# In the first stage of layer 0, the second parts of 31 weight blocks by accumulating DMA in place of subtractions on the vector engine and Pool

## The chip, the cores and the metric

One core of one Trainium2 chip runs the whole kernel in one launch. The metric is the device time of a launch in microseconds; smaller is better. The engines are named as in the profile: PE (matmuls), PEld (its weight loads), DVE (vector engine), ACT (scalar engine), POOL (GpSimd) and SP, which here only issues DMAs.

## The reference

A two-layer decoder step in float32 for a prompt group (512 tokens) and a sample group (8 x 4 tokens) with shared weights, width 1024. What matters here is the first part of layer 0 and the memory keys and values:

```python
def _conformer_conv(u, buf, w_in, b_in, dw, dw_b, ln_g, ln_b, w_out):
    h = jnp.einsum('bld,de->ble', u, w_in) + b_in               # 1024 -> 2048
    g = h[..., :D_MODEL] * jax.nn.sigmoid(h[..., D_MODEL:])
    padded = jnp.concatenate([buf.astype(g.dtype), g], axis=1)
    c = lax.conv_general_dilated(padded, dw[:, None, :], ...) + dw_b   # causal, depthwise, 31 taps
    ...                                                          # LayerNorm of c -> n
    s = jax.nn.silu(n).astype(u.dtype)
    return jnp.einsum('bld,de->ble', s, w_out), padded[:, -CONV_BUF:]

def _mem_kv(mem, w_k, w_v):                                      # 256 memory rows, per layer
    k = jnp.einsum('bmd,de->bme', mem, w_k)
    v = jnp.einsum('bmd,de->bme', mem, w_v)
```

After it come cross-attention and an MLP, then layer 1 (a state-space mixer, attention, MLP) and a final norm. None of that is touched.

## The kernel before

**Precision.** Products are made in fp32r. Each operand is split in two parts: `h`, its fp32r rounding, and `l`, what the rounding left over. A product is three passes over PE: h·h, l·h and h·l (weights named first). So a weight block that arrives by DMA as 128x1024 float32 (512 KB) needs two tiles of the same size before PE can finish with it.

**Blocks and buffers.** All weights are cut in such blocks. SP loads them in the order of use into six staging tiles `wst` (`load_upto`, line 162). `prep_block` makes both parts into one of only three tiles `whl` (128 x 2 x 1024): ACT copies `wst` into the first half (line 168 through the helper on line 136; the first part), then DVE, or Pool for the blocks in the set `lpool`, subtracts: second half = `wst` minus first half (line 172; the second part). A tile `whl` is free again when PE has finished the block that used it. So while PE works on block n, block n+1 is ready or nearly so, and block n+2 is prepared into the tile that block n-1 left.

**The first stage.** It runs from the start to about 240 us and consumes in this order: `in` 0 and 8 (first projections); `k` 0 to 2 (memory keys); then for i = 1 to 7 the pair `a`i, `b`i (blocks `in` i and `in` 8+i, 48 matmuls of 272 columns each); then `k` 3 to 7 (24 matmuls of 256 columns) and eight `v` blocks (12 matmuls of 512 columns), named here v00 to v03 and v10 to v13; then the output projection `cout`. The order is written out by hand in the string `PLAN`. Between those blocks stand:

- `g`i: DVE reads the two PSUM results (lines 520, 522), ACT takes the sigmoid, DVE multiplies, SP stores.
- The depthwise convolution. Channel tiles 0, 3 and 6 are done on DVE (31 operations of 0.77 us each, line 697), handed out in small portions between the other steps. Tiles 1, 2, 4, 5 and 7 are done on PE as banded matrix products: four steps a tile (`10`, `11`, ... `73`, 18 short matmuls each, line 677). Pool builds the band matrix of the step after next (line 650), ACT moves each step's result out of PSUM (line 136). All four results of a tile lie in one PSUM bank, `aux[1]`. Pool adds the finished tiles up (line 619); those of PE first go through DRAM (`ud`, `yd`).
- `L1` to `L3`: a LayerNorm over channels. PE sums (709), DVE subtracts the mean (718), ACT squares, DVE and Pool add the squares (730, 724), PE sums again with a few columns (282), woven between the matmuls of v blocks, DVE takes the reciprocal root (311 to 320), PE spreads it (328).

Each engine runs its own instructions in the order in which the program issues them. An engine that waits holds up all that stands behind it. Of SP, ACT and Pool, the three that issue DMAs, this holds for their DMAs too.

Of the kernel before, what the change touches and what calls it, by code (L numbers as in the profile page):

```python
# [7 lines left out]
F32R = mybir.dt.float32r  # L8
I32 = mybir.dt.int32
AF = mybir.ActivationFunctionType  # L10
ALU = mybir.AluOpType
# [37 lines left out]
BLOCK = {b: i for i, b in enumerate(block_order())}  # L49
# [8 lines left out]
class Trunk:  # L58
# [13 lines left out]
    def __init__(self, nc, tc, pool, psum, I, O):  # L72
        self.nc, self.tc, self.I, self.O = nc, tc, I, O
        self.pool, self.psum = pool, psum
        t = lambda name, *shape: pool.tile([P, *shape], F32, name=name)
# [27 lines left out]
        self.late = []  # L103
        self.lpool = {("k", 0, o) for o in range(1, 3)} | {("v", 0, 0, 3)} | {("v", 0, 1, k) for k in range(4)} | {("cout", o) for o in range(2)}
        self.lpool |= {b for b in self.KV1[1] + self.KV1[2][:2]}


    def ring(self, d):
# [56 lines left out]
    def prep_block(self, b, i, eng=None):  # L165
        t = self.whl.popleft()
        src = self.wst[i % self.NST]
        self.act(t[:, 0].bitcast(F32R), src, AF.Copy)
        if eng is None:
            eng = self.nc.gpsimd if b in self.lpool else self.nc.vector  # L170
        self.hl[b] = t
        eng.tensor_sub(t[:, 1].bitcast(F32R), src, t[:, 0])  # L172

    def pop_all(self):
# [2055 lines left out]
```

## Time and profile before

| | |
|---|---|
| time, median of 3 runs (lowest, highest) | 1548.17 us (1548.09, 1550.21) |
| time of the profiled execution | 1549.96 us |
| its span | 1548.2 us |
| busy: PE, PEld | 1498.7 us, 1452.3 us |
| busy: DVE, ACT, POOL | 1031.3 us, 672.1 us, 193.3 us |
| second parts by DVE, whole span | 149 of 128x1024, 1262 ns mean |
| second parts by Pool, whole span | 19, 2385 ns mean |
| weight loads from SP | 231 of 512 KB, median 4.3 us from issue to landing |

The span is the profiled execution as the trace sees it; 1.8 us of its time lie around it. Busy PE is pipelined time: matmuls overlap, so a busy PE can still be slower than its peak. Idle time in brackets in a timeline row is the idle time of that engine just before the row, with what released it.

### The profile page before, as it was taken

How to read it: one execution, taken by the hardware profiler on the slowest of the kernel's cores; microseconds unless marked ns; L12 is line 12 of the kernel's file. 1: busy time of each engine (PE TensorE's matmuls, PEld its weight loads, DVE VectorE, ACT ScalarE, POOL GpSimd, SP SyncE). 2: the span in 40 equal slices, each digit the busy share in tenths (PEclk: the TensorE clock that was granted, in tenths of full speed). 3: DMA queues.
4: the chain of work that ended last, by engine and by line, in shares of the span. 5: the costliest groups of instructions: out<-in, count | busy, mean ns of one | idle time of the engine just before them, and what ended most of it. 6: DMA issues, size and time to landing. Idle time of an engine off the chain costs nothing.

```text
span 1548.2 us, 29378 instructions
## 1 busy us (share of the span) xinstructions
PE 1498.7 (97%) x11949; PEld 1452.3 (94%) x11949; DVE 1031.3 (67%) x2106; ACT 672.1 (43%) x1262; POOL 193.3 (12%) x155
## 2 busy tenths in 40 slices
PE   8999979999999999999999999999999999999996
PEld 8999969988999999999998889998899999999996
DVE  6997877544577666666756974553479677585855
ACT  6122354333345433565434443343357445272542
POOL 2545451000000000000102760000000000000001
PEclk9999989999999999999999999999999999999998
DMA  7333425363323434333577975336322414141211
GB/s 277 123 90 106 141 112 203 141 256 123 107 73 102 148 134 133 134 133 107 178 259 230 323 241 199 110 137 252 143 69 82 137 55 150 43 140 52 90 47 59
DMA packets 90809, 218.21 MB, mean 141 GB/s; under 512 B 12305, under 2 KB 42785, under 8 KB 86577
## 3 DMA queue, kind: packets, MB, share of 16 engines
q1 hardware_dynamic: 87440, 211.06, 40.1%
q10 hardware_dynamic: 3168, 5.18, 0.9%
q8 instruction: 94, 1.54, 0.4%
q14 instruction: 43, 0.34, 0.1%
q0 software_dynamic: 64, 0.08, 0.0%
HBM read 186.48 MB, written 29.80 MB: 140 GB/s over the span
## 4 chain that ended last, share of the span: by engine, by line
PE 81%; DVE 12%; DMA 2%; issue 2%; ACT 2%; POOL 2%; SPq 0%; DVEq 0%; POOLq 0%; ACTq 0%
PE banks L210 45%; PE banks L1398 12%; PE banks L1290 10%; DVE banks L697 2%; PE banks L462 2%; PE banks L951 2%; PE banks L887 2%; DMA wst<-in_w 1%; PE banks L677 1%; PE banks L445 1%; DVE whl L172 1%; PE banks L968 1%; PE banks L871 1%; PE banks L222 1%; PE banks L1377 1%
## 5 line engine op out<-in xcount | busy, mean ns | idle before, releaser
L210 PE MATMUL banks<-slot,whl 128*128 128x272 f32 x6264 | 803.6, 289 | 5.5 <-ACT slot L136 2.3
L210 PEld LDWEIGHTS banks<-slot,whl 128*128 128x128 f32 x6264 | 792.6, 188 | 10.6 <-issue 4.1
L136 ACT ACTIVATE whl<-wst 128x1024 fp32r<-128x1024 f32 (+1 forms) x236 | 218.7, 931 | 133.4 <-PE banks L1398 47.8
L172 DVE TENSOR_TENSOR whl<-wst,whl 128x1024 fp32r<-128x1024 f32 x149 | 187.5, 1262 | 96.7 <-ACT whl L136 94.0
L1398 PE MATMUL banks<-slot,whl 128*128 128x272 f32 x912 | 120.2, 288 | 0.5 <-DVE rt L1311 0.5
L136 ACT ACTIVATE slot<-banks 128x512 fp32r<-128x512 f32 (+7 forms) x132 | 60.3, 480 | 137.8 <-PE banks L210 42.2
L1398 PEld LDWEIGHTS banks<-slot,whl 128*128 128x128 f32 x912 | 116.7, 188 | 0.7 <-DVE rt L1311 0.7
L1290 PE MATMUL banks<-slot,whl 128*128 128x272 f32 x756 | 97.2, 288 | 0.9 <-DVE tmp L1408 0.9
L1290 PEld LDWEIGHTS banks<-slot,whl 128*128 128x128 f32 x756 | 95.6, 188 | 1.1 <-ACT whl L136 1.1
L136 ACT ACTIVATE slot<-x,vec 128x544 fp32r<-128x544 f32 (+2 forms) x50 | 35.2, 728 | 109.0 <-DVE x L2022 44.2
L1408 DVE TENSOR_TENSOR tmp<-banks,rb 128x544 f32<-128x544 f32 x30 | 21.7, 724 | 83.0 <-PE banks L1398 83.0
L1398 PE MATMUL banks<-slot,arena_mlp 128*128 128x272 f32 x528 | 71.5, 288 | 0.4 <-DVE rt L1311 0.4
L697 DVE SCALAR_TENSOR_TENSOR banks<-slot,vec,banks 128x512 f32<-128x512 f32 x90 | 67.9, 754 | 2.6
L1398 PEld LDWEIGHTS banks<-slot,arena_mlp 128*128 128x128 f32 x528 | 68.2, 188 | 0.6 <-DVE rt L1311 0.6
L1480 POOL MEMSET slot<- 128x128 f32 x1 | 0.2, 205 | 546.9 <-PE banks L1290 546.9
L1290 PE MATMUL banks<-slot,arena_mlp 128*128 128x272 f32 x504 | 65.3, 288 | 0.4 <-DVE acc L1325 0.4
L1290 PEld LDWEIGHTS banks<-slot,arena_mlp 128*128 128x128 f32 x504 | 63.9, 188 | 0.7 <-DVE acc L1325 0.6
L136 ACT ACTIVATE tmp<-x 128x544 f32<-128x544 f32 x40 | 25.9, 648 | 65.0 <-DVE x L1094 39.7
L136 ACT ACTIVATE tmp<-banks 128x544 f32<-128x544 f32 x32 | 19.9, 623 | 76.5 <-PE banks L210 76.5
L420 POOL TENSOR_TENSOR slot<-slot,slot 128x512 fp32r<-128x512 f32 x4 | 6.1, 1559 | 371.4 <-ACT slot L136 371.4
L677 PE MATMUL banks<-slot,arena_mem 128*128 128x128 f32 (+2 forms) x360 | 46.1, 285 | 6.4 <-POOL arena_mem L650 3.3
L172 POOL TENSOR_TENSOR whl<-wst,whl 128x1024 fp32r<-128x1024 f32 x19 | 45.2, 2385 | 55.9 <-ACT whl L136 55.9
(281 smaller groups left out, 2030.4 us busy)
## 6 DMA issues: line engine op xcount, KB each, us to landing
wst<-in_w SPq DMA_DIRECT2D x231, 512.0 KB, 4.3
arena_att<-in_kc SPq DMA_DIRECT2D x16, 1024.0 KB, 4.8
arena_att<-in_vc SPq DMA_DIRECT2D x16, 1024.0 KB, 5.3
tab<-arena_prep SPq DMA_DIRECT2D x24, 512.0 KB, 3.9
arena_s<-tab SPq DMA_DIRECT2D x8, 768.0 KB, 5.5
arena_s<-tab SPq DMA_DIRECT2D x8, 512.0 KB, 6.3
arena_s<-tab SPq DMA_DIRECT2D x12, 256.0 KB, 5.5
x<-in_x SPq DMA_DIRECT2D x8, 272.0 KB, 6.0
```

The source lines that it names most:

```text
L136: self.nc.scalar.activation(out, in_, func, **kw)
L172: eng.tensor_sub(t[:, 1].bitcast(F32R), src, t[:, 0])
L210: self.nc.tensor.matmul(ps[:, c, :HALF], w, x[:, c * HALF : c * HALF + HALF], start=first and n == 0, stop=last and n == len(seq) - 1)
L222: self.nc.tensor.matmul(ps[:, c, :HALF], self.w8(b, kt)[wi], rhs[kt][xi].bitcast(F32R)[:, c * HALF : c * HALF + HALF], start=first and kt ...
L462: nc.tensor.matmul(ps[m], self.memt(2 * kp + k2, xi)[:, m * 128 : m * 128 + 128], t[:, wi, k2 * 512 : k2 * 512 + 512], start=kp == 0 and k ...
L677: nc.tensor.matmul(o[:, s:], mat(n)[:, s * 128 : s * 128 + 128], x[:, : 128 - s], start=s == 0, stop=s == 8)
L697: nc.vector.scalar_tensor_tensor(A, win(k), w(k), A, op0=ALU.mult, op1=ALU.add)
L887: nc.tensor.matmul(o, qs[qi], ks[ki], start=e == 0 and i == 0, stop=e == 1 and i == 2)
L951: nc.tensor.matmul(ps[e], vs[vi], xs[xi], start=m == 0 and i == 0, stop=m == 1 and i == 2)
L1290: nc.tensor.matmul(bank, u[:, wi, k * 128 : k * 128 + 128], x[k][xi].bitcast(F32R), start=n == k == 0, stop=n == 2 and k == 3)
L1398: nc.tensor.matmul(ps[:, c, :HALF], us[kt // 4][:, wi, kt % 4 * 128 : kt % 4 * 128 + 128], M["h"][kt][xi].bitcast(F32R)[:, c * HALF : c * ...
L1408: job("V", 0.7, lambda: V.tensor_mul(self.c2(t), self.psv(ps), self.c2(self.rb)), [*bk, "rb"], [("t", o % 2)])
```

## The change

For 31 blocks (the 14 `in` blocks of the pairs, `k` 1 to 7, all eight `v` blocks of layer 0 and `cout` 0 and 1) the subtraction is gone. In its place ACT writes the negated first part into the second half of the tile, and a DMA that Pool issues reads the block from DRAM a second time and adds it there: second half = -h + w. Of the 31, 22 were subtracted by DVE and 9 by Pool. `in` 0, `in` 8 and `k` 0 stay with DVE, and so does every block after `cout` 1.

```diff
@@ __init__
+        self.ldma = {("in", i + 8 * g) for i in range(1, 8) for g in range(2)} | {("k", 0, o) for o in range(1, 8)}
+        self.ldma |= {("v", 0, n, k) for n in range(2) for k in range(4)} | {("cout", o) for o in range(2)}
@@ prep_block
         self.hl[b] = t
+        if b in self.ldma:
+            self.act(t[:, 1].bitcast(F32R), t[:, 0], AF.Copy, scale=-1.0)
+            self.nc.gpsimd.dma_start(t[:, 1].bitcast(F32R), self.I["w"][BLOCK[b]], accum_op=ALU.add)
+            return
         eng.tensor_sub(t[:, 1].bitcast(F32R), src, t[:, 0])
```

Six lines are added above `tensor_sub` and two of them in `__init__`, so line numbers of the new kernel are larger by 2 up to there and by 6 behind it: 172 becomes 178, 650 becomes 656, and the new DMA is line 176.

How this moves instructions is shown at three places. The first is DVE between `g`2 and `g`3, about 68 to 84 us in the trace. Line 697 is the convolution of tile 0, 633 and 636 sum its sample columns, 520 and 522 open `g`3. Before:

```order
L633 TENSOR_REDUCE slot_798<-slot_632 128x16
L633 TENSOR_REDUCE slot_798<-slot_633 128x16
L636 TENSOR_SCALAR slot_631<-slot_798,vec 128x4x8
L697 SCALAR_TENSOR_TENSOR banks<-slot_496,vec,banks 128x512 x3
L172 TENSOR_TENSOR whl_83<-wst_80,whl_83 128x1024
L697 SCALAR_TENSOR_TENSOR banks<-slot_496,vec,banks 128x512 x7
L633 TENSOR_REDUCE slot_874<-tmp_86 128x16
L633 TENSOR_REDUCE slot_874<-tmp_87 128x16
L636 TENSOR_SCALAR slot_554<-slot_874,vec 128x4x8
L172 TENSOR_TENSOR whl_81<-wst_75,whl_81 128x1024
L520 TENSOR_TENSOR slot_932<-banks,rb 128x544
L522 TENSOR_TENSOR slot_931<-banks,rb 128x544
```

DVE at the same place in the changed kernel:

```order
L639 TENSOR_REDUCE slot_806<-slot_638 128x16
L639 TENSOR_REDUCE slot_806<-slot_639 128x16
L642 TENSOR_SCALAR slot_637<-slot_806,vec 128x4x8
L703 SCALAR_TENSOR_TENSOR banks<-slot_500,vec,banks 128x512 x10
L639 TENSOR_REDUCE slot_883<-tmp_86 128x16
L639 TENSOR_REDUCE slot_883<-tmp_87 128x16
L642 TENSOR_SCALAR slot_559<-slot_883,vec 128x4x8
L526 TENSOR_TENSOR slot_942<-banks,rb 128x544
L528 TENSOR_TENSOR slot_941<-banks,rb 128x544
```

Both subtractions have left DVE's queue; nothing else moved.

The second place is Pool from the last but one addition of a convolution tile (`acc`) on, about 174 to 204 us; line 650 builds a band matrix. Before:

```order
L619 TENSOR_TENSOR acc_84<-acc_84,slot88_1303 128x544
L650 TENSOR_TENSOR arena3072_mem_208<-istk_64,slot31_233 128x1152
L619 TENSOR_TENSOR acc_84<-acc_84,slot95_1452 128x544
L650 TENSOR_TENSOR arena3072_mem_208<-istk_64,slot31_233 128x1152
L172 TENSOR_TENSOR whl0_81<-wst3_78,whl0_81 128x1024
L172 TENSOR_TENSOR whl1_82<-wst4_79,whl1_82 128x1024
L172 TENSOR_TENSOR whl2_83<-wst5_80,whl2_83 128x1024
L714 MEMSET slot119_1956 128x256
```

Pool at the same place in the changed kernel; the DMAs are, from the top, those of `k` 6, `k` 7, v00, v01, v02, v03, v10 and v11:

```order
L176 DMA whl1_82<-in_w 128x1024
L625 TENSOR_TENSOR acc_84<-acc_84,slot88_1317 128x544
L656 TENSOR_TENSOR arena3072_mem_208<-istk_64,slot31_233 128x1152
L625 TENSOR_TENSOR acc_84<-acc_84,slot95_1468 128x544
L176 DMA whl2_83<-in_w 128x1024
L656 TENSOR_TENSOR arena3072_mem_208<-istk_64,slot31_233 128x1152
L176 DMA whl0_81<-in_w 128x1024
L176 DMA whl1_82<-in_w 128x1024
L176 DMA whl2_83<-in_w 128x1024
L176 DMA whl0_81<-in_w 128x1024
L176 DMA whl1_82<-in_w 128x1024
L176 DMA whl2_83<-in_w 128x1024
```

The DMA of `k` 7 stands behind two additions and a build, and that of v00 behind another build; `k` 6, `k` 7 and v00 to v02 were subtracted by DVE before, so Pool had no part in them.

The third place is ACT in the LayerNorm, about 195 to 204 us, where the copy of block v12 stands between the two halves of the squares (`acc` and `slot`). Before:

```order
L136 ACTIVATE whl2_83<-wst5_80 128x1024
L136 ACTIVATE acc_84<-slot50_554 128x544
L136 ACTIVATE slot112_1949<-slot56_631 128x544
L136 ACTIVATE slot113_1950<-slot64_778 128x544
L136 ACTIVATE slot114_1951<-slot72_955 128x544
L136 ACTIVATE whl0_81<-wst0_75 128x1024
L136 ACTIVATE slot115_1952<-slot79_1135 128x544
L136 ACTIVATE slot116_1953<-slot88_1303 128x544
```

ACT at the same place in the changed kernel:

```order
L138 ACTIVATE whl2_83<-wst5_80 128x1024
L138 ACTIVATE whl2_83<-whl2_83 128x1024
L138 ACTIVATE acc_84<-slot50_559 128x544
L138 ACTIVATE slot112_1976<-slot56_637 128x544
L138 ACTIVATE slot113_1977<-slot64_786 128x544
L138 ACTIVATE slot114_1978<-slot72_965 128x544
L138 ACTIVATE whl0_81<-wst0_75 128x1024
L138 ACTIVATE whl0_81<-whl0_81 128x1024
L138 ACTIVATE slot115_1979<-slot79_1147 128x544
L138 ACTIVATE slot116_1980<-slot88_1317 128x544
```

Each copy of a weight block is now followed by a negation, ahead of the squares.

## Rows read from the trace of the kernel before

**Rows 1.** Busy time of each engine in the stretch from the start of `a`1 to `k` 3: stretch, length, busy us and instruction counts, then the granted PE clock (1.00 is 2.4 GHz), the DMA share and GB/s.

```profile
36.80:161.90 125.10, 118.64 (x943) 118.03 (x944) 112.27 (x145) 26.59 (x39) 62.53 (x38) 0.98 0.34 103
```

**Rows 2.** Timeline of PE alone: start, length, instruction, and in brackets the idle time ahead of it. L677 is a step of the convolution on PE, L445 a `k` block.

```profile
63.86 2.24 PE L677 MATMUL banks<-slot,arena_mem 128*128 128x128 f32 x18 [0.55 <-ACT slot L136]
...
80.08 2.16 PE L677 MATMUL banks<-slot,arena_mem 128*128 128x128 f32 x18
84.81 3.67 PE L677 MATMUL banks<-slot,arena_mem 128*128 128x128 f32 x18 [2.56 <-issue]
...
137.85 2.27 PE L677 MATMUL banks<-slot,arena_mem 128*128 128x128 f32 x18 [0.97 <-POOL arena_mem L650]
...
158.58 3.34 PE L677 MATMUL banks<-slot,arena_mem 128*128 128x128 f32 x18 [2.32 <-POOL arena_mem L650]
161.59 3.69 PE L445 MATMUL banks<-arena_mem,whl 128*128 128x256 f32 x24
...
167.04 3.06 PE L445 MATMUL banks<-arena_mem,whl 128*128 128x256 f32 x24
```

**Rows 3.** Timeline of all engines ahead of the two longest of these idle times: a subtraction and the opening of `g`3 on DVE, its sigmoid on ACT, and the moving of step `13` out of PSUM; then the opening of `g`7 and the moving of step `51`.

```profile
81.44 1.54 DVE L172 TENSOR_TENSOR whl<-wst,whl 128x1024 fp32r<-128x1024 f32 x1 [0.33 <-ACT whl L136]
...
82.91 0.71 DVE L520 TENSOR_TENSOR slot<-banks,rb 128x544 f32<-128x544 f32 x1
...
83.70 0.75 ACT L136 ACTIVATE slot<-slot,vec 128x544 f32<-128x544 f32 x1 [2.29 <-issue]
...
84.36 0.35 ACT L136 ACTIVATE slot<-banks,slot 128x128 f32<-128x128 f32 x1
...
156.68 0.72 DVE L520 TENSOR_TENSOR slot<-banks,rb 128x544 f32<-128x544 f32 x1
...
158.09 0.35 ACT L136 ACTIVATE slot<-banks,slot 128x128 f32<-128x128 f32 x1
```

**Rows 4.** Groups of instructions by line in the first 240 us: busy us, mean ns of one, idle time before them. The first two are the copies and DVE's subtractions of weight blocks, the third Pool's subtractions, the last one of the two DMAs that Pool issues in this kernel (64 KB, 128 rows), as long as it held Pool.

```profile
L136 ACT ACTIVATE whl<-wst 128x1024 fp32r<-128x1024 f32 x35 | 36.9, 1054 | 20.7 <-DMA wst<-in_w 7.1 <-issue 6.6 <-PE banks L462 4.4
L172 DVE TENSOR_TENSOR whl<-wst,whl 128x1024 fp32r<-128x1024 f32 x26 | 36.1, 1387 | 14.2 <-ACT whl L136 14.2
...
L172 POOL TENSOR_TENSOR whl<-wst,whl 128x1024 fp32r<-128x1024 f32 x9 | 21.4, 2380 | 35.4 <-ACT whl L136 35.4
...
L372 POOL DMA_DIRECT2D ident<-in_ident x1 | 0.7, 707 | 0.8 <-POOLq L2207 0.8
```

**Rows 5.** The loads of weight blocks (512 KB) in the first 240 us: time from issue to landing.

```profile
DMA to landing us min/median/max: 3.3/4.5/7.0
```

**Rows 6.** DMA issues over the whole span: loads of cached keys, 1024 KB each, median us from issue to landing.

```profile
arena_att<-in_kc SPq DMA_DIRECT2D x16, 1024.0 KB, 4.8
```

**Rows 7.** The same view as rows 1 for the stretch of the `k` and `v` blocks, and for its busiest 5 us; the two columns at the end are the DMA share and GB/s.

```profile
160.00:205.00 45.00, 45.00 (x304) 41.63 (x303) 34.26 (x42) 21.98 (x38) 26.96 (x16) 0.97 0.59 194
195.00:200.00 5.00, 5.00 (x23) 4.08 (x22) 3.02 (x5) 3.26 (x5) 4.41 (x4) 1.00 1.01 407
```

**Rows 8.** Timeline of all engines around `k` 6 to v02: Pool's additions and a build, `k` 7 on PE (24 matmuls), v00 to v02 on PE (36 matmuls), ACT's copy of v02, and seven loads of weight blocks that SP issues one behind the other.

```profile
174.70 1.35 POOL L619 TENSOR_TENSOR acc<-acc,slot 128x544 f32<-128x544 f32 x1 [4.92 <-DVE banks L697]
...
176.00 2.13 POOL L650 TENSOR_TENSOR arena_mem<-istk,slot 128x1152 f32<-128x1152 f32 x1
...
178.10 2.33 POOL L619 TENSOR_TENSOR acc<-acc,slot 128x544 f32<-128x544 f32 x1
...
181.59 3.10 PE L445 MATMUL banks<-arena_mem,whl 128*128 128x256 f32 x24
...
186.45 8.65 PE L462 MATMUL banks<-whl,arena_mem 128*128 128x512 f32 x36
...
187.55 1.06 ACT L136 ACTIVATE whl<-wst 128x1024 fp32r<-128x1024 f32 x1 [0.46 <-ACT slot L136]
...
191.03 8.00 SPq L162 DMA_DIRECT2D wst<-in_w  x7
```

**Rows 9.** Timeline in the LayerNorm: ACT's copy of v12 and the second four squares, Pool's subtraction of v12, the first small sums of the second group on PE, and one small operation of the reciprocal root on DVE.

```profile
200.19 1.05 ACT L136 ACTIVATE whl<-wst 128x1024 fp32r<-128x1024 f32 x1
201.14 2.28 ACT L136 ACTIVATE slot<-slot 128x544 f32<-128x544 f32 x4
...
201.87 2.40 POOL L172 TENSOR_TENSOR whl<-wst,whl 128x1024 fp32r<-128x1024 f32 x1
...
209.38 0.38 PE L282 MATMUL banks<-ones,slot 128*128 128x2 f32 x2 [2.68 <-DVE slot L730]
...
216.19 2.28 DVE L318 TENSOR_TENSOR sm_t<-sm_y 128x5 f32<-128x5 f32 x1
```

**Rows 10.** The chain of work that ended last, in order of time, in the LayerNorm: two of the four additions of squares on DVE, and a small operation of the reciprocal root.

```profile
202.11 2.75 DVE slot L730
...
207.77 0.73 DVE slot L730
...
218.91 0.18 DVE sm_t L318
```

**Rows 11.** Timeline at the start of the stage: ACT's copy of `k` 2, PE on `k` 1, and PE from `a`1 on.

```profile
25.51 1.06 ACT L136 ACTIVATE whl<-wst 128x1024 fp32r<-128x1024 f32 x1 [0.93 <-DMA wst<-in_w]
...
27.88 3.07 PE L445 MATMUL banks<-arena_mem,whl 128*128 128x256 f32 x24
...
36.85 24.45 PE L210 MATMUL banks<-slot,whl 128*128 128x272 f32 x192 [1.33 <-DVE slot L528]
```

## The prediction

> **What bounds the kernel now.** I read the busy time by stretches first. Between `a`1 and `k` 3 PE is busy 118.6 of 125.1 us and DVE 112.3 [rows 1]: two engines are nearly full at once, so the question is which of them makes the other wait. PE's own timeline answers it. In that stretch it has four idle times, of 0.55, 2.56, 0.97 and 2.32 us, and all of them end at a convolution step [rows 2]. The first is the plain case: a step follows another with no gemm between, both write the bank `aux[1]`, and the second waits until ACT has moved the first one's result out. I take 0.55 us as the floor of such a pair. The two long ones are put down to "issue" and to Pool, but I read them as the same wait: step `13`'s result is moved out at 84.36, right behind the sigmoid of `g`3 at 83.70, which waits for DVE's line 520 at 82.91, which stands behind a subtraction at 81.44; step `20` starts 0.10 us after the move [rows 2, 3]. Around 156.68 it is the same with `g`7 [rows 3]. So DVE's backlog reaches PE through ACT's order, and 1 to 3 us at a time.
>
> From `k` 3 on PE has no such waits until the LayerNorm, where it waits for DVE (2.68 us at 209.38) [rows 9].
>
> **The change part by part.** D is the time from Pool's issue of an accumulating DMA to its landing. No row shows such a DMA, and nearly every cost hangs on D.
>
> *D, from both sides.* The fastest plain load of this size took 3.3 us, the median 4.5, the slowest 7.0 [rows 5]; a load of twice the size takes 4.8 [rows 6]. An accumulation reads the block and its destination and writes the destination, so I take no less than 3.3 us, and up to 9 (the slowest load, and 2 us for a second pass). I take 6.5, near the slow end: 4.5 for the load, 1.3 for a second pass (512 KB at the 407 GB/s of the busiest stretch [rows 7]), and 0.7 that Pool needs to issue [rows 4]. For v02 alone I take 8.5, since it would be in flight with SP's seven loads in a row from 191.03 on [rows 8], which keep the DMA engines at a share of 1.01 [rows 7].
>
> *What a block costs now.* The copy takes 1.05 us on ACT, the subtraction 1.39 on DVE or 2.38 on Pool [rows 4]. Then: copy 1.05, negation, which I put at 1.05 as well (same size, same engine), and D. The second part is ready 1.05 + D, or 7.55 us, after the copy, not 1.4 to 2.4. What hides this is the two-block lead. Between gemms with a convolution step it is some 16 us (two gemms of 24.45 / 4 and two steps of 2.2 [rows 2, 11]) and hides all of it. Between `k` blocks with their steps it is about 12 us, between bare `v` blocks under 6.
>
> *Gain 1: the idle times of PE before `k` 3.* DVE loses 22 subtractions, some 30 us over the stage, and by `g`3 it is ahead by far more than the 2.7 us it lags. The gaps shrink to their floor: 2.56 - 0.55 = 2.0, 0.97 - 0.55 = 0.4, 2.32 - 0.55 = 1.8. PE also came out of the two long ones slowly: 18 matmuls took 3.67 and 3.34 us instead of 2.16, and a `k` block 3.69 instead of 3.06 [rows 2]: 1.5 + 1.2 + 0.6. Together -7.5 us. The cover is Pool's: it must still build the matrices in time, with a DMA of about 0.7 us more for each gemm. Pool is busy 62.5 of 125.1 us there [rows 1], so I cost this at nothing.
>
> *Cost 1: the start.* The wait for ACT behind `k` 2's copy (25.51 [rows 11]) grows by 1.05 to 1.25 us, so `k` 1 starts at 29.3 instead of 27.88. Its copy is done at 24.6 (25.51 less the idle 0.93), its negation at 25.6, its second part at 25.7 + D = 32.2. PE can do a third of the block (1.0 us) before it needs that: it waits from 30.3 to 32.2. The other two thirds, the spreading (0.6) and `k` 2 (3.0) bring `a`1 to 37.7 against 36.85 [rows 11]: +0.9 (D of 4.5: -0.9, as the second wait behind DVE's subtraction is gone too; D of 9: +3.4).
>
> *Cost 2: `k` 7.* Its DMA stands in Pool's queue behind the two additions and the build of [rows 8]: 174.70 + 1.35 + 2.13 + 1.35 (the last without the disturbance that made it 2.33) gives 179.5. The first addition waits for a tile from DRAM that PE's step sets off, so this doesn't come earlier. PE starts `k` 7 at 181.59 and needs the second part a third later, 182.6: wait D - 3.1 = 3.4 us. Behind the DMA, in Pool's queue, stand only the last build and the `v` blocks' DMAs.
>
> *Cost 3: v02.* Its tile comes free with `k` 7, and ACT copies it at 187.55, behind the last convolution step [rows 8]. Copied 188.6, negated 189.7, landed 189.7 + D. The three blocks take 8.65 us from 186.45 [rows 8], so v02 begins at 192.2 and needs the second part after two matmuls, 192.6: wait D - 2.9 = 5.6 us at 8.5. Behind v02 on PE stand the LayerNorm's sums, so this shifts all that follows.
>
> *Gain 2: the LayerNorm.* Of DVE's four additions the first two took some 2.7 us each, the others 0.73; the slow ones lie beside Pool's subtractions, such as that at 201.87 [rows 9, 10]. That is 4.0 us, and the negation of v12 ahead of the second squares takes 1.05 back. One operation of the root took 2.28 us, another of its kind 0.18, again beside a subtraction on Pool [rows 9, 10]: -2.1. But then v12 is late: copied 201.2, negated 202.3, landed 202.4 + D = 208.9. PE comes to it at 206.7 (209.38 less the 2.68 it waited) and does two matmuls; it waits 1.7 us instead of 2.7, and the small sums woven into that block wait with it. Net -0.9 - 2.1 = -3.0 (D of 4.5: -4.5; D of 9: -0.5).
>
> *Cost 4: the clock.* After 2.56 us of idle time PE's next 18 matmuls took 1.5 us longer [rows 2]. Two new waits of that size: +3.0.
>
> *Sum:* -7.5 + 0.9 + 3.4 + 5.6 - 3.0 + 3.0 = **+2.4 us**. The profiled execution took 1549.96 us with a span of 1548.2; the median of the runs, 1548.17, is 1.8 below it. The sum moves the span, so the median goes from 1548.2 to **1550.6 us**.
>
> **A page beside it.** The loads of 512 KB landed in 4.5 us [rows 5]. The Trainium skill, "DMA: Bandwidth & Descriptors", section on the anatomy of one DMA on Pool's path, fits 2.0 us plus the bytes over 436 GB/s: 3.2 us for this size, by my estimate from it. With that D the sum would be some 12 us below zero. The trace's loads, from SP, are slower than that fit, and no run here shows it for Pool's.
>
> **The rivals.** *It lands like a plain load* (D = 4.5 throughout). Then the waits at `k` 7 and v02 are 1.4 and 1.6 us, too short to cost much clock (after 0.97 us PE lost 0.1 [rows 2]), the start gains 0.9 and the LayerNorm 4.5: -7.5 - 0.9 + 1.4 + 1.6 + 0.2 - 4.5 = -9.7, 1538.5 us. For it: the 1 MB loads, which move as many bytes as both reads, need only 4.8 us. Against it: a read that must come back before the write can start.
>
> *The DMA engines fill up* (slower). From 160 to 205 us the DMA share is 0.59 [rows 7], which leaves 18.4 us of 45. Ten accumulations (`k` 5 to v12) fall in there. One pass over 512 KB takes 1.29 us at 407 GB/s. Three passes each (read, read, write, not overlapped) are 38.7 us, 20 too many, and no order of issue hides that: -7.5 + 0.9 + 20 - 2.1 = +11, 1559.5 us. It decides from about 2.4 passes on, where the overrun (31 less 18.4) passes the 12 us of costs 2 to 4. For it: the share of 1.01 at 195 to 200 us. The Trainium skill, same page, section "Issuing engines are not separate DMA queues", says that DMAs of every issuing engine run on the same 16 DMA engines and interleave; by that rule SP's loads and Pool's DMAs must share. Against it: the passes may well overlap.
>
> *Pool becomes the engine that PE waits for.* If a DMA holds Pool for 2 us or more, not 0.7, the builds for steps `43` and `52` come late (the first was already, by 0.4 us): twice 1.3, twice 1.5 of clock, and gain 1 is mostly lost: +2.4 + 5.6 = 1556 us. Pool's half-empty time speaks against it.
>
> **How the numbers follow.** Forecast (D about 6.5, within some 3 us of zero or a little above): 0.38. Plain-load D: 0.28. Full DMA engines: 0.24. Pool: 0.10. A measurement of this kernel can tell about 0.2%, 3.1 us, from no change. Faster by more than that: the plain-load case and a corner of the forecast (D below 5.5), 0.33. Slower: the two slow rivals and the forecast's upper part, 0.42. Between: 0.25. The forecast's own range is 1543 to 1556. As cases of both signs hold much of the chance, the range takes in both ends: 1538 (the plain-load sum) to 1561 (D of 9: -7.5 + 3.4 + 5.9 + 8.1 - 0.5 + 3 = +12.4).
>
> **What would show it.** Right: PE without idle time over 0.6 us before `k` 3, `g`3's and `g`7's line 526 right behind the end of `b`3 and `b`7; waits of PE for a DMA into `whl` at `k` 7 and in v02 and v12; additions of squares at 0.73 us. D itself is the row of Pool's DMA issues. Wrong: PE waiting for builds (Pool), for a DMA between the gemms before `k` 3 (D above 14), or no waits at `k` 7 and v02 (D below 3). If the gaps before `k` 3 stay although DVE is idle, my reading of them was wrong and 7.5 us are missing.

## The result and the profile after

| | median, lowest to highest | |
|---|---|---|
| before | 1548.43 us (1548.09 to 1550.21, 4 runs) | |
| after | 1562.62 us (1560.97 to 1564.99, 4 runs) | ratio 1.009, 95% interval 1.0073 to 1.0108 |

The change makes the kernel slower by 0.9%. The forecast of 1550.6 us was wrong, and the result lies above its range too, by 1.6 us. The profiled execution of after took 1564.99 us with a span of 1563.2, 15.0 us more than the span before. All of it arises in the first stage. PE's timeline of after, with the rows that answer to [rows 2, 8, 9, 11]; L683 is a convolution step, L451 a `k` block, L468 the `v` blocks, L715 the LayerNorm's first sums:

```profile
32.73 3.78 PE L451 MATMUL banks<-arena_mem,whl 128*128 128x256 f32 x16 [1.23 <-DMA whl<-in_w]
...
137.47 2.24 PE L683 MATMUL banks<-slot,arena_mem 128*128 128x128 f32 x18 [0.55 <-ACT slot L138]
...
156.38 2.24 PE L683 MATMUL banks<-slot,arena_mem 128*128 128x128 f32 x18 [0.55 <-ACT slot L138]
158.38 3.06 PE L451 MATMUL banks<-arena_mem,whl 128*128 128x256 f32 x24
...
172.89 2.91 PE L451 MATMUL banks<-arena_mem,whl 128*128 128x256 f32 x16 [3.60 <-DMA whl<-in_w]
175.60 3.02 PE L683 MATMUL banks<-slot,arena_mem 128*128 128x128 f32 x18
...
189.48 3.79 PE L451 MATMUL banks<-arena_mem,whl 128*128 128x256 f32 x16 [5.04 <-DMA whl<-in_w]
193.06 2.83 PE L683 MATMUL banks<-slot,arena_mem 128*128 128x128 f32 x18
...
204.93 4.04 PE L468 MATMUL banks<-whl,arena_mem 128*128 128x512 f32 x10 [2.96 <-DMA whl<-in_w]
...
220.40 0.73 PE L468 MATMUL banks<-whl,arena_mem 128*128 128x512 f32 x2 [2.81 <-DMA whl<-in_w]
```

Between `a`1 and `k` 3 the four gaps are at their floor (0.51 to 0.55 us), as forecast. Behind `k` 3 PE waits in `k` 5, `k` 7, v02 and v11, each time where the second part is first used: after 8 of the 24 matmuls of a `k` block, after 2 of the 12 of a `v` block. (The last row is v11's: its DMA, issued at 211.74, landed after 8.6 us. The forecast and the expectations name v12 there; v12 made nobody wait.) After the waits the next matmuls are slow: 16 of `k` 7 in 3.79 us, where e13 below needs 2.15.

How long the accumulating DMAs took from issue to landing (minimum, median, maximum), in the stretches from 10, 50, 160 and 205 us on; there are 6, 12, 8 and 5 of them:

```profile
DMA to landing us min/median/max: 5.8/7.6/8.6
...
DMA to landing us min/median/max: 5.3/5.7/8.4
...
DMA to landing us min/median/max: 5.7/9.1/10.5
...
DMA to landing us min/median/max: 5.4/5.8/8.6
```

Over all 31 the median is 6.7, close to the D of 6.5 that the forecast took. But it is 5.7 where the forecast found good cover and 9.1 where it found little. Why it differs is in the busy times by stretches (columns as in [rows 1, 7]: the granted clock, the DMA share and GB/s stand last):

```profile
165.00:170.00 5.00, 4.29 (x38) 4.08 (x36) 4.89 (x8) 2.40 (x5) 1.61 (x2) 1.00 0.99 258
170.00:175.00 5.00, 2.11 (x14) 2.11 (x15) 2.95 (x6) 2.69 (x3) 0.00 (x0) 0.90 0.95 209
...
180.00:185.00 5.00, 4.44 (x39) 4.23 (x37) 2.79 (x1) 3.17 (x6) 5.00 (x5) 1.00 0.39 61
185.00:190.00 5.00, 0.52 (x2) 0.52 (x3) 0.11 (x1) 0.92 (x1) 1.52 (x2) 0.76 1.04 241
190.00:195.00 5.00, 5.00 (x28) 5.00 (x27) 0.43 (x1) 0.66 (x2) 0.00 (x0) 0.55 0.89 185
195.00:200.00 5.00, 5.00 (x28) 4.18 (x27) 0.00 (x0) 3.60 (x5) 0.85 (x1) 1.00 0.21 71
200.00:205.00 5.00, 2.04 (x10) 1.33 (x8) 0.00 (x0) 3.00 (x3) 1.73 (x3) 0.97 0.97 207
205.00:210.00 5.00, 5.00 (x16) 4.01 (x17) 0.00 (x0) 1.00 (x1) 0.00 (x0) 0.69 1.03 280
210.00:215.00 5.00, 4.55 (x20) 3.40 (x19) 4.16 (x7) 4.46 (x7) 3.14 (x4) 1.00 1.05 310
215.00:220.00 5.00, 2.58 (x12) 1.74 (x10) 3.88 (x6) 4.94 (x10) 1.67 (x2) 1.00 1.05 308
220.00:225.00 5.00, 4.60 (x19) 3.99 (x20) 0.00 (x0) 0.89 (x3) 0.87 (x1) 0.68 1.08 256
225.00:230.00 5.00, 5.00 (x19) 4.33 (x17) 0.00 (x0) 3.90 (x5) 0.88 (x1) 0.50 0.21 43
```

In 165 to 175, 185 to 190 and from 200 to 225 us the 16 DMA engines are busy with hardly a pause (shares of 0.95 to 1.08), and move only 207 to 310 GB/s; the full stretch before moved 407 [rows 7]. The granted clock falls towards half (1.2 GHz) behind the waits (0.55 in 190 to 195), is back at 1.00 in 180 to 185 and 195 to 200, and is at half again in 225 to 230 (0.50), where PE does the LayerNorm's small sums.

The chain of waits of after, in order of time, names what was in flight there:

```profile
163.88 9.47 DMA yd<-slot
...
174.81 2.13 DMA slot<-yd
...
181.79 5.28 DMA whl<-in_w
...
199.15 5.74 DMA whl<-in_w
...
211.74 8.61 DMA whl<-in_w
```

The store of `yd`, one finished convolution tile on its way through DRAM, took 9.47 us; the same store took 2.5 before, and 4.6 in e3 below, where none of the 31 DMAs is issued. Pool's additions wait for its reload, and `k` 7's DMA stands behind them. (The chain follows that DMA for 5.28 us only; it landed after 7.6, at 189.44, and PE went on at 189.48.) On DVE the four additions of the LayerNorm take 2.9 us in all, without the slow ones of [rows 10]:

```profile
L736 DVE TENSOR_TENSOR slot<-slot,slot 128x544 f32<-128x544 f32 x4 | 2.9, 726 | 1.1 <-ACT slot L138 0.8
```

### The profile page after: what moved, and what is told of

It reads as the page before. It is cut to its first block, busy times and chain, and to the rows that moved or that the text cites. A ratio compares the mean times of both kernels' runs of the same rounds, so it can differ in the third digit from the quotient of the medians.

```text
span 1563.2 us, 29426 instructions
## 1 busy us (share of the span) xinstructions
PE 1508.0 (96%) x11949; PEld 1460.0 (93%) x11949; DVE 998.6 (64%) x2084; ACT 705.3 (45%) x1293; POOL 194.1 (12%) x177
## 3 DMA queue, kind: packets, MB, share of 16 engines
q1 hardware_dynamic: 87440, 211.06, 39.9%
## 4 chain that ended last, share of the span: by engine, by line
PE 86%; DVE 6%; DMA 3%; issue 2%; ACT 1%; POOL 0%; SPq 0%; DVEq 0%; POOLq 0%; ACTq 0%
PE banks L216 49%; PE banks L1404 12%; PE banks L1296 10%; PE banks L683 2%; PE banks L468 2%; DMA whl<-in_w 2%; PE banks L893 2%; PE banks L957 2%; PE banks L228 1%; PE banks L974 1%; PE banks L877 1%; PE banks L1383 1%; PE banks L451 1%; DVE banks L1959 1%; ACT slot L138 1%
## 5 line engine op out<-in xcount | busy, mean ns | idle before, releaser
L178 DVE TENSOR_TENSOR whl<-wst,whl 128x1024 fp32r<-128x1024 f32 x127 | 156.4, 1235 | 89.8 <-ACT whl L138 86.9
L703 DVE SCALAR_TENSOR_TENSOR banks<-slot,vec,banks 128x512 f32<-128x512 f32 x90 | 67.9, 755 | 2.9
L251 DVE TENSOR_TENSOR slot<-tmp,slot 128x544 fp32r<-128x544 f32 x32 | 23.2, 725 | 42.3 <-ACT slot L138 42.3
L138 ACT ACTIVATE rt<-rt 128x272 f32<-128x272 f32 (+1 forms) x92 | 45.3, 501 | 9.5 <-DVE rt L1348 4.7
```

The costliest lines, as they stand in the source:

```text
L138: self.nc.scalar.activation(out, in_, func, **kw)
L251: self.nc.vector.tensor_sub(l.bitcast(F32R), src_h if src_l is None else src_l, h)
L703: nc.vector.scalar_tensor_tensor(A, win(k), w(k), A, op0=ALU.mult, op1=ALU.add)
```

## The experiments

Theory A: an accumulation costs time of the 16 DMA engines, all transfers share it, and a landing is late by what is in flight. Theory B: an accumulating DMA has a fixed long way, whatever its size, and only the lead of two blocks is too short. Theory C: `k` 7 is late because of Pool's order. The expectations of e1 to e4 still go by three other names: late landing (the lead is too short), full DMA engines (theory A at its strongest) and ACT (the negations hold it up). Each run is compared with the kernel before on the same chip (its median was 1550.79 us for e1 to e4, 1550.31 for e5 to e8, 1550.18 for e9 to e12 and 1550.37 for e13 and e14), so ratios are what can be set side by side.

**e1 and e2: one half of the change each.**

```diff
 e1: self.ldma = {("in", i + 8 * g) for i in range(1, 8) for g in range(2)}
 e2: self.ldma = {k 1 to 7} | {v, all eight} | {cout 0, 1}
```

> Only the 14 in blocks take the accumulating DMA; k, v and cout blocks are subtracted by DVE and Pool as before. Late landing (the second parts of k and v blocks land later than the two-block lead covers, those of in blocks do not): the gaps of PE before k 3 close and nothing is paid, about 7 us below the kernel before, 1541.5. Full DMA engines (the 31 accumulations and the loads together need more than the 16 engines have, all through the stage): part of the gain is lost to late loads and stores, 1546 to 1550. ACT (the 31 extra negations delay what ACT does for PE): about 1545.

> The other half: only k 1 to 7, the eight v blocks and cout 0 and 1 take the accumulating DMA, the in blocks are subtracted by DVE as before. Late landing: all of the loss without the gain, 14 + 7 above the kernel before, about 1569. Full DMA engines: with 14 accumulations fewer the engines are less full and the loss shrinks, at most 1563. ACT: half of the negations, half of the loss, about 1555.

e1: 1544.12 us, ratio 0.9964 (0.9951 to 0.9976), **faster than both kernels**. PE never waits for an accumulating DMA. The time is 2.6 us above what late landing gave and below the range of full engines. One gap is left above its floor, behind ACT:

```profile
153.23 2.24 PE L682 MATMUL banks<-slot,arena_mem 128*128 128x128 f32 x18 [1.71 <-ACT slot L137]
```

e2: 1567.8 us, ratio 1.0111 (1.0084 to 1.0138). All the waits of after are there (2.24 at `k` 5, 4.67 at `k` 7, 3.69 at v02), and of the gain a part only: of the gaps ahead of `k` 3 that of 2.56 us stays (2.47), that of 2.32 is at its floor. So the two halves have opposite signs. The time is late landing's (1569); full engines gave 1563 at most.

**e3 and e4: no transfer; a transfer without the addition.** In e3 the DMA is left out, so the second parts stay the negated first parts. In e4 it overwrites the second part with the block, and adds nothing.

```diff
-            self.nc.gpsimd.dma_start(t[:, 1]..., self.I["w"][BLOCK[b]], accum_op=ALU.add)
 e3: (nothing)
 e4:         self.nc.gpsimd.dma_start(t[:, 1]..., self.I["w"][BLOCK[b]])
```

> All 31 blocks get the negated first part from ACT, and the accumulating DMA is left out, so the second parts stay negated first parts. What is left is the relief of DVE and Pool and the cost of the negations. Late landing and full engines alike: no waits for a DMA into whl, gaps closed, LayerNorm some 3 us shorter: 1536 to 1539. ACT: the loss stays, 1550 or more.

> As the changed kernel, but Pool's DMA overwrites the second part with the block and does not add, so the second part is the block itself: one read and one write per DMA, the same queue and the same waits. Late landing: the landing time falls from 6.7 to about 5 us and the waits at k 5, k 7 and v02 shrink with it, about 1548 to 1552. Full DMA engines: the same DMAs at half the engine time, no waits for engines, 1541 to 1546. If Pool's way of issuing is what is slow and not the addition: no change, 1560.

e3: 1537.5 us, ratio 0.9915 (0.9898 to 0.9931). Freeing DVE and Pool is worth 13 us, and behind `a`1 the negations cost PE nothing that shows, which rules out ACT as the cause. e4: 1550.23 us, ratio 1.0002 (0.9992 to 1.0011). The transfer as such eats the 13 us, and the addition some 14 more. This is late landing's range again (1548 to 1552); full engines gave 1541 to 1546. Theory A is what is left of full engines after that: a share that delays, not a sum that overruns.

**e5 and e13: the same DMAs with fewer bytes.** e5 adds the first 512 of 1024 columns, e13 the first 32; the rest of each second part stays the negated first part.

```diff
-  dma_start(t[:, 1]..., self.I["w"][BLOCK[b]], accum_op=ALU.add)
 e5:   dma_start(t[:, 1, :512]..., self.I["w"][BLOCK[b]][:, :512], accum_op=ALU.add)
 e13:  dma_start(t[:, 1, :32]..., self.I["w"][BLOCK[b]][:, :32], accum_op=ALU.add)
```

> Left out: the accumulating DMAs add the block's first 512 columns only, so that the other half of each second part stays the negated first part. Theory A (an accumulation costs time of all 16 DMA engines, about 2.9 us for a block, and what is late waits for engine time): half the bytes take half the engine time, about 1.45 us each, landings fall from a median of 6.7 us to about 4, the waits at k7 and v02 lose more than half of their 5.0 and 3.0 us, k5's goes, and the time lies half way between e3's 1537.5 and the changed kernel's 1562.6: about 1550. Theory B (a DMA that reads its destination, adds and writes has a fixed way to go, whatever its size, and the lead is too short for it): landings stay at 5.5 us or more, the waits lose under a third, and the time is 1557 to 1561.

> Left out: the accumulating DMAs add the block's first 32 of 1024 columns only; the rest of each second part stays the negated first part. All 31 DMAs are issued from the same places and waited for by the same matmuls, with 16 KB each. The shortest landings so far, 5.3 us for 512 KB and 3.7 for 256 KB, make 1.6 us for 256 KB and leave 2.1 to 2.2 us for a DMA with next to no bytes. Theory A (the cost goes with the bytes): landings of 2.2 to 3 us, no wait at k5, k7, v02 or v12 over 1 us, k3 to the LayerNorm's sums in 33 to 35 us (e3: 32.75, after: 50.43), 1538 to 1542. Theory B (a fixed way of an accumulating DMA, or Pool's 0.87 us for each issue): the waits at k7 and v02 keep 2 us or more, 1547 or above.

e5: 1550.72 us, ratio 1.0000 (0.9991 to 1.0010). e13: 1541.25 us, ratio 0.9949 (0.9932 to 0.9965), with all 31 issues and all their waits in place. The landings of e13, over the whole stage:

```profile
DMA to landing us min/median/max: 2.3/3.1/6.8
```

The line of the DMA queue that carries Pool's DMAs (packets, MB, share of 16 engines' span), for e13, e5, e4 and after:

```profile
q0 software_dynamic: 4528, 0.59, 0.6%
```

```profile
q0 software_dynamic: 4528, 8.21, 3.2%
```

```profile
q0 software_dynamic: 4528, 16.34, 3.4%
```

```profile
q0 software_dynamic: 4528, 16.34, 5.8%
```

Times its span and over 31 DMAs, each share is the time of all 16 engines that one DMA takes. Beside it the landing of the `yd` store issued between 160 and 165 us (4.6 in e3), and the cost over e3, as the difference of the ratios:

| | 16 engines, us each | shortest / median landing, us | `yd` store, us | over e3 |
|---|---|---|---|---|
| e13, 16 KB added | 0.30 | 2.3 / 3.1 | 5.6 | 0.34% |
| e5, 256 KB added | 1.60 | 3.7 / 4.8 | 6.8 | 0.85% |
| e4, 512 KB, not added | 1.70 | 3.5 / 4.9 | 7.6 | 0.87% |
| after, 512 KB added | 2.92 | 5.3 / 6.7 | 9.5 | 1.75% |

e5 and e4 differ in bytes and in operation, but take nearly the same engine time, land alike and cost alike. That speaks against B: a fixed way, whatever the size, and Pool's issue hold little (at most e13's 0.34%). These columns alone would also fit a DMA that is long by itself and shares nothing. The store speaks for A: it has the same 256 KB in every run and ACT issues it, yet it lands the later the more engine time Pool's DMAs take. e13's time is in the range that A gave; `k` 7 still waited 1.88 us, and the stretch from `k` 3 to the sums, 35.92 us, is 0.9 longer than A's upper end.

**e6 and e7: one block more of lead**, with four tiles of two-part weights (and four staging tiles, for the room), in after and, as control, in before.

```diff
-    NST, NHL, NSLOT, AHEAD = 6, 3, 48, 4
+    NST, NHL, NSLOT, AHEAD = 4, 4, 48, 4
```

> The changed kernel with four tiles of two-part weights instead of three (and four staging tiles instead of six, for the room), so that a block is begun three blocks ahead and not two. To be compared with the next run, not with the kernel before. Theory A (engine time is short from 160 to 230 us): an earlier start moves the same transfers, the waits at k5, k7 and v02 to v12 fall by less than half of their 14.9 us and the first stage ends at most 7 us earlier. Theory B (only the lead is too short): all these waits but k1's go, PE keeps its clock, and the first stage ends some 15 to 20 us earlier than in the changed kernel (LayerNorm's root at about 210 us instead of 230).

> The kernel before with four tiles of two-part weights and four staging tiles, the control of the run above. No wait of PE before k3 comes from the lead, so both theories expect the first stage within 2 us of the kernel before; four staging tiles instead of six can cost waits for loads in later stages, up to 10 us. Theory B expects the run above to be 5 to 12 us faster than this one, theory A slower or within 5 us.

e6: 1558.35 us, ratio 1.0055 (1.0041 to 1.0070). e7: 1553.97 us, ratio 1.0032 (1.0019 to 1.0045). Between the two only 0.2% is left of after's 0.9%; the first stage of e6 ends 1.6 us after e7's, where after's ends 15.0 after before's. (The control's first stage ended 2.5 us later than before's, a little more than expected.) PE's timeline of e6:

```profile
181.72 4.20 PE L683 MATMUL banks<-slot,arena_mem 128*128 128x128 f32 x18 [5.35 <-POOL arena_mem L656]
...
191.25 8.65 PE L468 MATMUL banks<-whl,arena_mem 128*128 128x512 f32 x36
...
203.93 0.70 PE L715 MATMUL banks<-slot,ones 128*128 128x272 f32 x2 [3.57 <-DMA slot<-yd]
```

and its chain of waits:

```profile
164.23 9.65 DMA yd<-slot
...
197.41 6.32 DMA slot<-yd
```

Neither theory had it right alone. All waits for a two-part block are gone but 0.55 us at `k` 1, as B said; but the landings are no shorter (median 6.7), and two waits for `yd` stand in their place, as slow transfers of others, which is A's. The root of the LayerNorm is spread at 222.81 instead of 234.95 us, 12 us sooner, between what A and B expected.

**e9: the additions that wait for the reload on DVE, not Pool.**

```diff
-            self.conv_sum(i, g, nc.gpsimd)
+            self.conv_sum(i, g, nc.vector if i == 5 else nc.gpsimd)
-        self.conv_sum(i, out, nc.gpsimd)
+        self.conv_sum(i, out, nc.vector if i == 6 else nc.gpsimd)
```

> The changed kernel with the three additions of partial convolution sums that wait for the reload of yd in this part (tile 5's and tile 6's) on DVE and not on Pool. In the changed kernel k7's negation was done at 174.45 us, but its DMA was issued at 181.79, behind two of these additions in Pool's queue, which waited 9.53 us for the reload. Theory C (Pool's order makes k7 late): the DMA goes out at about 175, k7's wait of 5.0 us and the slow matmuls behind it (some 2.5 us) go, v02 keeps a wait of 3 us or more: 1555 to 1558 against 1562.6. Theory A alone (the transfers are too slow, whenever they are issued): k7 still waits 2 us or more, 1560 or above. If DVE, which now waits for the reload itself, becomes late, a wait for DVE shows at the last convolution steps.

A miss: 1564.41 us, ratio 1.0093 (1.0078 to 1.0108), `k` 7 waits 4.22 us. DVE's timeline, with the rest of a convolution tile (L703) behind the addition:

```profile
178.18 0.73 DVE L625 TENSOR_TENSOR acc<-acc,slot 128x544 f32<-128x544 f32 x1 [6.74 <-DMA slot<-yd]
178.82 0.75 DVE L703 SCALAR_TENSOR_TENSOR banks<-slot,vec,banks 128x512 f32<-128x512 f32 x1
```

and ACT's, where `k` 7's copy stands behind moving out that tile:

```profile
179.66 0.69 ACT L138 ACTIVATE slot<-banks,vec 128x512 f32<-128x512 f32 x1 [10.32 <-DVE banks L703]
180.25 1.05 ACT L138 ACTIVATE whl<-wst 128x1024 fp32r<-128x1024 f32 x1
```

DVE waited for the reload in Pool's place, and held ACT with it. `k` 7's DMA left no earlier (182.69 against 181.79 us). The run doesn't refute that Pool's queue held `k` 7's DMA in after; it shows that the late reload reaches `k` 7 by whichever engine adds.

**e10 and e11: `k` 5 and `k` 6 back on DVE**, with three tiles and with four.

```diff
-  {("k", 0, o) for o in range(1, 8)}
+  {("k", 0, o) for o in (1, 2, 3, 4, 7)}
```

> The changed kernel with k5 and k6 subtracted on DVE as before, 29 accumulating DMAs left. The DMAs of k5 and k6 were issued at 162.69 and 166.70 us, around the store of yd at 163.88, which took 9.47 us to land, in a stretch with a DMA share of 0.95 to 0.99. Theory A: the store lands in under 6 us, its reload and Pool's additions come 3 us or more earlier, k5's wait of 3.6 us goes; k7 then waits as long as before or less, since PE is there earlier too: 1556 to 1559. Theory B (each late block is late by its own way alone): the store still takes 9 us, only k5's 3.6 us and its clock go, and k7's wait grows by as much: 1561 to 1563.

> Four tiles (as e6) and k5 and k6 subtracted on DVE. In e6 the waits for two-part blocks were gone but for 0.5 us, and what stood in their place was 5.35 us for a matrix that Pool built late behind the reload of yd, whose store took 9.7 us, and 3.57 us for the next reload. If the accumulations of k5 and k6 make the store late, the 5.35 shrinks to 2 or less, the clock stays, and the time is 5 to 7 us below e6's 1558.35: 1552 to 1554. If something else makes the store late (SP's loads of weights), it stays within 2 us of e6.

e10: 1562.49 us, ratio 1.0073 (1.0057 to 1.0090); e11: 1558.42 us, ratio 1.0061 (1.0046 to 1.0076), not below e6. Both miss A's number; e10's time is in the range that B gave. The `yd` store did land sooner, as A said, after 6.4 us in e10 and 2.6 in e11 (after 9.5, e6 9.7). In e11 its reload then took up to 6.8 us, and PE still waited 3.24 us for the build behind it. What PE waited for in e10 is this:

```profile
179.46 2.27 PE L683 MATMUL banks<-slot,arena_mem 128*128 128x128 f32 x18 [1.87 <-POOL arena_mem L656]
...
186.63 3.78 PE L451 MATMUL banks<-arena_mem,whl 128*128 128x256 f32 x16 [3.95 <-DMA whl<-in_w]
...
203.13 4.04 PE L468 MATMUL banks<-whl,arena_mem 128*128 128x512 f32 x10 [3.51 <-DMA whl<-in_w]
```

`k` 5's 3.60 us are gone; a new wait for a build (1.87) and 0.55 us more at v02 take part of it. From `k` 3 to the sums e10 is 3.4 us shorter than after (47.05 against 50.43), but it came to `k` 3 1.6 us later. A gain of this size is not resolved by these runs.

**e14: the `v` blocks back on DVE and Pool.**

```diff
-        self.ldma |= {("v", 0, n, k) for n in range(2) for k in range(4)} | {("cout", o) for o in range(2)}
+        self.ldma |= {("cout", o) for o in range(2)}
```

> The changed kernel with the eight v blocks subtracted on DVE and Pool as before; k1 to k7, the in and the cout blocks by accumulating DMAs. It parts the costs of k5 to k7 from those of v. The prediction's terms for v were 5.6 us of wait at v02 and 3.0 us gained in the LayerNorm. Theory A (transfers share the engines in the whole stretch): v02's wait of 2.96 us and its slow matmuls go (4 to 5 us), k7's wait stays at 4 to 5 us, the LayerNorm takes 24 to 25 us as in e1: about 1557. If the cost sat mainly in v, it falls to the level of e1, 1546 or less; if mainly in k, it stays at 1561 or above.

1557.54 us, ratio 1.0049 (1.0032 to 1.0066), the time that A gave. `k` 5 and `k` 7 wait as in after (3.46 and 5.52 us), v02 no longer; the LayerNorm took 19.58 us, 5 less than expected. The trace shows where: with `v` back on Pool the four additions are slow as before (7.35 us), but the reciprocal root on DVE takes 2.8 us instead of 7.2, as `cout` 0 and 1 are no longer subtracted on Pool beside it. By the ratios, from e1's 0.9964 on, the `k` and `cout` blocks cost 0.85% and the `v` blocks another 0.41%: both do harm, the `k` blocks more.

**e8 and e12: can more than the `in` blocks be kept?**

```diff
 e8:  self.ldma = {("in", ...)} | {("k", 0, 3), ("k", 0, 4)}
 e12: self.ldma = {("in", ...)} | {("k", 0, 3)} | {("v", 0, 1, k) for k in range(3)}
```

> Accumulating DMAs for the 14 in blocks and for k3 and k4 alone, which in the changed kernel landed after 5.6 and 5.3 us and made nobody wait. In e1 an idle time of 1.71 us was left at 153.2, behind ACT, beside DVE's subtractions for k3 and k4. Both theories: that one shrinks to 0.55, no new wait of PE, 1 to 2 us below e1's 1544.1, 1542.5. If these two DMAs take engine time that others want (theory A at its strongest), the yd store's and the wst loads' landings grow and nothing is gained: 1544 to 1546.

> Accumulating DMAs for the 14 in blocks, k3, and v10, v11 and v12, whose subtractions on Pool lie beside DVE's four additions of the LayerNorm (7.28 us before and in e8, 3.22 in the changed kernel). The additions take about 3.2 us. Against e1's 1544.1: minus 2.7 us of PE's wait for them, minus some 3.5 of its wait for the root, plus a wait for v12, whose DMA is in flight with SP's seven loads (8 us or so to land): if that is under 3 us, 1541; if theory A's full engines make it 5 us or more, 1544 to 1547.

e8: 1544.02 us, ratio 0.9965 (0.9953 to 0.9977): the same as e1. The gap of 1.71 us shrank to 0.55 as expected, but PE waited 0.89 us for an `in` block and 1.70 for a build instead, and the `yd` store took 6.4 us (4.2 in e1): the outcome of theory A at its strongest. e12: 1546.32 us, ratio 0.9976 (0.9967 to 0.9985), the second of its two outcomes: the additions take 3.21 us as expected, but the three DMAs beside SP's loads landed after 8.7, 9.9 and 10.4 us, and PE waited for v10's:

```profile
199.72 5.07 PE L468 MATMUL banks<-whl,arena_mem 128*128 128x512 f32 x14 [4.48 <-DMA whl<-in_w]
```

## Why the prediction was wrong

The stretches of the stage, from the starts of PE's rows (`a`1, `k` 3, the LayerNorm's sums, the spreading of its root, `cout` 2), us:

| | `a`1 at | to `k` 3 | to the sums | to the root | to `cout` 2 |
|---|---|---|---|---|---|
| before | 36.85 | 124.74 | 33.35 | 24.59 | 20.16 |
| after | 40.26 | 118.12 | 50.43 | 26.14 | 19.75 |
| e3, no transfer | 39.86 | 117.95 | 32.75 | 16.56 | 21.99 |
| e13, 16 KB | 38.31 | 117.92 | 35.92 | 19.29 | 20.48 |
| e4, not added | 37.52 | 117.93 | 43.00 | 19.08 | 20.49 |
| e6, four tiles | 40.81 | 117.92 | 41.01 | 23.07 | 20.90 |
| e14, no `v` | 39.84 | 118.13 | 45.30 | 19.58 | 22.46 |

Before to after: +3.4 - 6.6 + 17.1 + 1.5 - 0.4 = +15.0 us, the whole difference of the spans.

- **Gain 1** (-7.5): right. The stretch lost 6.6 us, and the gaps went where and why it said. Every run with the `in` blocks by DMA has 4.3 us of it or more (e12, 120.46 us, has the least). Not all of it is theirs: e2, with the `in` blocks as before, needs 120.81, as its last gap is at the floor and the first has no slow matmuls behind it.
- **Cost 1** (+0.9): +3.4, and only partly the DMA's. `k` 1's DMA landed at 32.7, where the sum had 32.2, and PE waited 1.23 us for it. What the sum put at nothing is the clock behind that wait (0.56 in 30 to 35 us): up to `a`1 the matmuls lost 2.4 us. And `k` 0 began 1.4 us later than before, ahead of anything that the change touches. The start scatters, but not only by chance: with three tiles `a`1 starts at 35.77 to 36.85 us where `k` 1 and 2 are subtracted (before, e1, e8, e12), and at 37.52 to 42.45 where ACT negates them, in e3 too (39.86), which has no transfer. How much of that the negations cost is not shown; e7, which has none, but four tiles, starts `a`1 at 41.11.
- **Costs 2, 3 and 4** (3.4 + 5.6 + 3.0 = 12.0): 17.1, the largest miss. Measured are waits of 3.60 (`k` 5), 5.04 (`k` 7) and 2.96 us (v02), 11.6 in all, and 5.5 us of slow matmuls behind them: 1.6, 2.3 and 1.6 against the same matmuls at full clock. The clock's 3.0 was for two such waits, and there were three. That the two priced waits add up nearly right (9.0 forecast, 8.0 measured) is luck: `k` 7's DMA took 7.6 us, not 6.5, and v02's 5.7, not 8.5, as SP's seven loads were issued only behind it. The wait that was not foreseen is `k` 5's. "Between `k` blocks with their steps it is about 12 us" left room for a D of 6.5 there; `k` 5's DMA, issued at 162.69 in among SP's loads, the `yd` store and `k` 6's DMA, took 10.2.
- **Gain 2** (-3.0): +1.5. Its mechanism was right and its size too small: in e3 the stretch is 8.0 us shorter. The four additions went as priced (from 7.28 to 3.22 us), but the root had more than one slow operation: without subtractions on Pool it takes 2.8 us (e3, e14; 4.8 in after, beside another operation of Pool), not 7.2. What failed is the landing term. The sum had 1.7 us of wait at v12; PE waited 2.81 us for v11, which landed 8.6 us after an issue that was late already, and then did the small sums at half clock (0.50 at 225 to 230 us). The forecast's own figures said that a second part needs 7.55 us between bare `v` blocks with a lead under 6; it priced v02 and v12 and left out the others. The transfers cost 9.6 us in this stretch, from 16.56 to 26.14.

Of the 12.6 us between +2.4 and +15.0 costs 2 to 4 hold 5.1, gain 2 4.5, cost 1 2.5 and gain 1 0.9; the last stretch gives 0.4 back. So the step that failed is D as a fixed number (6.5, and 8.5 for v02 alone), and with it the delay of other transfers by the accumulations, which the sum put at nothing. Its median was right, but it is no property of the DMA: it was 5.3 to 5.7 us where little else moved and up to 10.5 where other transfers did. The three blocks of the LayerNorm and those around `yd` stood in the second kind of place.

Of the rivals, **full DMA engines** came nearest in time (1559.5) and in cause, yet not as it was put. It wanted an overrun of the sum over 45 us, from 2.4 passes on. The engines needed 2.92 us for an accumulation, some 2 passes of the 1.29 to 1.55 us that a load takes (1.55: after's loads, 39.9% of the span for 211.06 MB), and from 160 to 205 us their share was 0.77, not 1. In that stretch no sum overran; the bursts did, and they delayed transfers that had a waiter. The stretch behind it was full, with a share of 1.03 from 200 to 225 us: there SP's seven loads, issued from 200.17 on, took 6.0 to 17.2 us to land beside the accumulations of `v`. What the rival missed is that the loss needs no full stretch, only a queue ahead of a transfer with a short lead: e6 keeps the bytes and a full stretch (1.04 from 200 to 225 us) and hides the accumulations' landings, but for 0.55 us, with one block more of lead, and then waits for `yd`. **Plain-load D** fell with the landings; e4 shows that even it would only have come out even, since a plain load from Pool landed in 4.9 us, not 4.5, and shared the engines too. **Pool's own time** was not the cause: e13 has the same issues.

The Trainium skill, "DMA: Bandwidth & Descriptors", section "Issuing engines are not separate DMA queues", says that DMAs of scalar, sync and GpSimd run on the same 16 engines and interleave. The trace agrees: a store from ACT took 4.6 us beside SP's loads alone (e3) and 9.47 beside DMAs of Pool and SP. The Trainium skill, same page, section "Anatomy of one DMA — SWDGE (gpsimd) path", has a fit for a DMA of Pool, 2.0 us plus the bytes over 436 GB/s; the estimate from it is 3.2 us for 512 KB. e4's shortest, 3.5 us, is near it, but its median of 4.9 is not, and no accumulation of 512 KB took under 5.2 (the shortest, in e8).

What stays open: how the loss divides between lead and contention (e6 changes the staging tiles too, so its 0.2% over e7 holds for this lead and these tiles), and the scatter of the start. An estimate from the rows above: had each DMA landed in the shortest time, 5.3 us, from the issue that it had, the waits at `k` 7 and v02 would be 2.7 and 2.5 us and those at `k` 5 and v11 nothing, 5.2 of the measured 14.4 us. The rest would be contention, and of the issues some are late by contention too.

## What to carry to other kernels

Moving work from an engine to a DMA doesn't make it free: price it in time of the 16 DMA engines, and look at the DMA share in bursts of 5 us, not over the stage. Use it where the lead is long and the engine that it relieves holds up the others (the `in` blocks: -0.4%), and leave it where the lead is short or other transfers with a waiter are in flight. Removing one of several waits in such a stretch mostly hands the time to the next, so judge a fix by the length of the stretch, not by the wait that went away.

## What was not expected of the hardware

- Adding makes a DMA from Pool dearer: of 512 KB, 2.92 us of the 16 engines instead of 1.70, and 5.2 us to land at the least (e8) instead of 3.5.
- Pool is held for 0.87 us (median) by an accumulating DMA, whether it adds 16 KB or 512; a plain one of 512 KB held it 0.53 to 0.59.
- While the engines are full of accumulations and loads they move 207 to 310 GB/s by the profile's count, well under what a full stretch without accumulations reached (407 [rows 7], 405 in e3 at 190 to 195 us).
